# A matmul with layer normalisation: the fifth row tile's first quarter taken early, one quarter turned by VectorE, loads by quadrant

## The chip, the cores and the metric

The kernel runs on one core of a Trainium2 chip. The metric is the device time of one execution in microseconds, as the median of several runs. Five engines work side by side, each through its own queue of instructions: TensorE (PE) multiplies, VectorE (DVE) and ScalarE (ACT) work element by element, GpSimd (POOL) and SyncE (SP) issue most of the DMAs. Engines wait for one another by semaphores.

## The reference

With a and b of 2048 x 2048 in fp32:

```python
x = np.matmul(a, b)
mean = np.mean(x, axis=-1, keepdims=True)
var = np.var(x, axis=-1, keepdims=True)
normalized = (x - mean) / np.sqrt(var + eps)
return (gamma * normalized + beta).astype(np.float32)
```

Mean and variance of a row need the row's 2048 products complete, and the products need all of b.

## The kernel before

**Tiles.** Rows of a are cut into 16 row tiles of 128, numbered from 0, so tile 4 is the fifth. The columns of b are cut into 4 blocks of 512, and k into 16 k tiles of 128. A row tile has four *quarters* of k, of four k tiles each; (i, c) is quarter c of row tile i, and (i, q) is, for products, column block q of row tile i. One matmul (`mm`, L140) takes one k tile of one row tile as stationary operand, 128 x 128, and 512 columns of b, in fp16, and adds into one of the 8 PSUM banks. Row tiles 0 to 14 take 64 matmuls each, 960 in all; the last one has spans of its own (`products_last`).

**Ways to turn a.** The stationary operand needs k on the partitions. Row tiles 0 to 3 come as sixteen *pieces* (tile, quarter) of 128 x 512; each is cast to fp16 (`cast_first`), transposed by TensorE in four 128 x 128 steps into a PSUM bank (`turn_first`) and copied to `at` by VectorE (`keep_first`). Row tiles from 4 on are loaded so that each group of 32 partitions holds another 32-column part (`load_tile`: eight DMAs of 64 KB a half tile), cast by ScalarE (`cast_tile`), and turned in 32 x 32 blocks by VectorE (`transpose_part`, one quarter per instruction).

**Stages.** b arrives during the first 60 us, in left halves and right halves of each k tile (`load_b`), and is cast half by VectorE and half by ScalarE (`cast_left`, `cast_right`). Four row tiles work together meanwhile:

- the first K1 = 4 k tiles of the left two column blocks, then of the right two; the partial sums are put by in SBUF (`put_by`, ScalarE for even blocks, VectorE for odd ones);
- the other 12 k tiles of the left blocks, then of the right ones, each sum added to the part put by (`add_up`, VectorE), with its statistics (`stats`, VectorE) after it;
- then the loop over row tiles 4 to 14, 64 matmuls each, which also turns tile i + 2, normalises tile i - 1, and takes a half of one of the first four tiles (`normalise`: `centre` and `scale` on VectorE);
- the last row tile, with a shorter tail.

**Order.** The order of the work is written out by hand: the Python code is run once, and what it emits for an engine is that engine's queue, in that order. So a line that stands later in the code stands later in its engine's queue. The SP queue issues the loads of b and of row tiles 0 to 5, gamma, beta and the outputs; the POOL queue issues those of row tiles 6 to 15. A load also waits for a free buffer: `firstp` has 4 for a, `bigp` has 8 for b and the outputs.

**What the change touches.** The list of pieces (L89); the loads (L314 to L341); the end of the right first stage, where pieces 6 and 7 are turned (L409 to L426); the left second stage (L429 to L455), which turns pieces 8 to 15; the right second stage (L458 to L485), where tile 4's quarters are turned by VectorE among the additions and tile 5's after the statistics; and the loop (L487 to L508).

Of the kernel before, what the change touches and what calls it, by code (L numbers as in the profile page):

```python
# [9 lines left out]
FP32 = mybir.dt.float32  # L10
FP16 = mybir.dt.float16
# [4 lines left out]
def kernel(  # L16
# [16 lines left out]


    nc = tc.nc
    P = 128
# [15 lines left out]
    atp = ctx.enter_context(tc.tile_pool(name="atp", bufs=6))  # L52
    xpool = ctx.enter_context(tc.tile_pool(name="xpool", bufs=16))
    upool = ctx.enter_context(tc.tile_pool(name="upool", bufs=2))
# [33 lines left out]

    pieces = [(g, c) for c in range(4) for g in range(G)]  # L89

# [23 lines left out]

    def load_tile(i, h, queue):
        f = firstp.tile([P, 2, 4, P], FP32, tag="first", name=f"p{i}_{h}")
        for c in (0, 1):
            for q in range(4):
                queue.dma_start(  # L119
                    f[ds(32 * q, 32), c], a_pieces[q, 2 * h + c][:, ds(4 * i, 4)])  # L120
        tile_in[i, h] = f

    def cast_tile(i, h):
        a16 = a16p.tile([P, 2, 4, P], FP16, tag="a16", name=f"a{i}_{h}")
        nc.scalar.copy(a16, tile_in.pop((i, h)))  # L125
        tile_in[i, h] = a16

# [3 lines left out]
    def transpose_part(i, c):  # L131
        nc.vector.transpose(  # L132
            at[i][:, ds(4 * c, 4), :].rearrange("p t (j r) -> p j t r", r=32),
            tile_in[i, c // 2][:, c % 2].rearrange("p j (k t) -> p j t k", t=4),
        )
# [162 lines left out]
    with tc.manual_schedule(engines=order):  # L298
# [21 lines left out]
        for t in range(K1):  # L320
            load_b(t, 1)
            if t:
                load_first(K1 + t - 1)
        load_first(2 * K1 - 1)
        for t in range(K1, n_kt):
            load_b(t, 0)
            if K1 + t < n_kt:
                load_first(K1 + t)
        for t in range(K1, n_kt - 2):
            load_b(t, 1)  # L330
        load_tile(4, 0, nc.sync)
        for t in range(n_kt - 2, n_kt):
            load_b(t, 1)
        load_tile(4, 1, nc.sync)
        for h in (0, 1):
            load_tile(5, h, nc.sync)
        nc.sync.dma_start(gamma_b, gamma.unsqueeze(0).to_broadcast([P, N]))
        nc.sync.dma_start(beta_b, beta.unsqueeze(0).to_broadcast([P, N]))
        for i in range(6, n_mt):
            for h in (0, 1):  # L340
                load_tile(i, h, nc.gpsimd)  # L341

# [65 lines left out]
        bank(*late)  # L408
        cast_first(2 * K1 - 1)  # L409
        waits = list(range(K1))  # L410
        for j, (g, q) in enumerate(early):
            mm(g, q, K1 - 1, 0, K1)
            put_by(g, q)
            if j in (4, 6):
                n = K1 + j // 2
                turn_first(n)
                keep_first(n)
            if j in (1, 3, 5):
                mm(*late, waits.pop(0), 0, K1)
            if j == 2:  # L420
                cast_left(K1)
            if j == 5:
                cast_first(2 * K1)
        for t in waits:
            mm(*late, t, 0, K1)
        put_by(*late)  # L426


# [3 lines left out]
        for t in range(K1, n_kt - 3):  # L432
            n = K1 + t
            if t > K1:
                keep_first(n - 1)
            if K1 < t and n < n_kt:
                cast_first(n)
            cast_left(t + 1)
            for g, q in early[:5]:
                mm(g, q, t, K1)  # L440
            if n < n_kt:
                turn_first(n)
            for g, q in early[5:]:
                mm(g, q, t, K1)
        bank(*late)
        for t in range(n_kt - 2, n_kt):
            cast_left(t)
        for t in range(K1, n_kt - 3):
            mm(*late, t, K1)
        for j, (g, q) in enumerate(left):  # L450
# [7 lines left out]
        for g, q in right:  # L458
            bank(g, q)
        new_at(4)  # L460
        for t in range(K1 + 3, n_kt):
            if t == n_kt - 2:
                cast_tile(4, 0)
                transpose_part(4, 0)
                transpose_part(4, 1)
            cast_right(t)
            if t - K1 - 3 < len(left):
                stats(*left[t - K1 - 3])
        for t in range(K1, n_kt - 2):
            for g, q in right:  # L470
                mm(g, q, t, K1)
        cast_tile(4, 1)
        for j, (g, q) in enumerate(right):
            for t in (n_kt - 2, n_kt - 1):
                mm(g, q, t, K1)
            add_up(g, q)
            if j in (1, 3):
                transpose_part(4, 2 + j // 2)
        for g, q in right:
            stats(g, q)  # L480
        new_at(5)
        for c in range(4):
            if c % 2 == 0:
                cast_tile(5, c // 2)
            transpose_part(5, c)  # L485

        for i in range(G, last):  # L487
# [8 lines left out]
            for q in range(n_nb):  # L496
                bank(i, q)
                for t in range(n_kt):
                    mm(i, q, t)
                stats(i, q)  # L500
                if i + 2 < n_mt:
                    if q % 2 == 0:
                        cast_tile(i + 2, q // 2)
                    transpose_part(i + 2, q)
# [44 lines left out]
```

## Time and profile before

| | |
|---|---|
| median of 7 runs | 244.82 us (244.55 to 245.58) |
| the profiled execution's own time | 244.48 us |
| its span, first to last instruction | 242.7 us |
| TensorE busy | 232.6 us (96%) |
| VectorE busy | 197.5 us (81%) |
| ScalarE busy | 94.1 us (39%) |
| matmuls on row tiles 0 to 14 | 960 |
| transposes on TensorE (128 x 128) | 64 |
| turnings on VectorE, 0.689 us each | 48 |
| read from HBM, written | 35.65 MB, 16.78 MB |

Matmuls overlap in the pipeline, so a row's mean duration of one (379 ns) is longer than the time from one start to the next. A timeline line gives start and duration in microseconds, engine, line of the kernel, operation, output and input tile with shapes, how many instructions were merged, and in brackets the idle time before it with what ended it. Windows give, for each stretch, its length, busy time and number of instructions of TensorE, its weight loads, VectorE, ScalarE and GpSimd, then TensorE's granted clock as a share of the full one, the busy share of the DMA engines and GB/s.

### The profile page before, as it was taken

The page shows a single profiled execution, that of the slowest core. Times are in us where ns is not written, and L with a number is a line of the kernel's source. Part 1 is how long each engine was busy: PE and PEld are TensorE (multiplying, and loading weights), DVE is VectorE, ACT ScalarE, POOL GpSimd, SP SyncE. Part 2 cuts the span into 40 slices and gives each one's busy share as a digit, 9 for nine tenths or more (in the row PEclk, how much of TensorE's full clock was granted, in tenths as well). Part 3 has the DMA queues.
Part 4 walks back from the last instruction along what each step waited for, and adds up shares of the span by engine and source line. Part 5 has one row for each costly group of instructions (what it writes and reads, how often), then busy time and mean ns, then how long its engine had stood idle before and what let it go on. Part 6 is the DMA issues. An engine that isn't in the chain of part 4 may idle for free.

```text
span 242.7 us, 3388 instructions
## 1 busy us (share of the span) xinstructions
PE 232.6 (96%) x1137; PEld 108.5 (45%) x1137; DVE 197.5 (81%) x371; ACT 94.1 (39%) x167; POOL 89.2 (37%) x168
## 2 busy tenths in 40 slices
PE   8999999999999999999999999999999999999960
PEld 2445554444444444444444444444444444446440
DVE  1467865883599999998999899998999895966962
ACT  3474434443325130461909255370917391020020
POOL 0000000000776497798976707693670000000011
PEclk9999999999999999999999999999999999999996
DMA  6999999995989558586866726472584222030405
GB/s 177 402 404 402 399 402 409 406 328 170 258 218 314 161 171 274 188 281 131 259 205 230 224 97 242 166 276 86 209 214 185 90 86 89 35 138 0 176 0 173
DMA packets 22129, 52.66 MB, mean 217 GB/s; under 512 B 4448, under 2 KB 9056, under 8 KB 21856
## 3 DMA queue, kind: packets, MB, share of 16 engines
q1 hardware_dynamic: 16704, 41.74, 47.0%
q0 software_dynamic: 5120, 10.50, 16.9%
q8 instruction: 9, 0.15, 0.3%
q10 hardware_dynamic: 288, 0.21, 0.3%
q14 instruction: 8, 0.07, 0.1%
HBM read 35.65 MB, written 16.78 MB: 216 GB/s over the span
## 4 chain that ended last, share of the span: by engine, by line
PE 94%; DVE 3%; issue 0%; DVEq 0%
PE ps L141 84%; PE ps_last L230 6%; PE w_ps L306 3%; PE t_ps L109 2%; DVE x L154 1%; DVE c L287 1%; DVE at L113 0%; DVEq L544 0%; DVE b L86 0%; DVE ps_last L259 0%; DVE h L103 0%; DVE mv_last L272 0%; DVE bnst_last L249 0%; DVE warm L299 0%; DVE rs L173 0%
## 5 line engine op out<-in xcount | busy, mean ns | idle before, releaser
L141 PE MATMUL ps<-b,at 128*128 128x512 f16 x960 | 210.6, 379 | 0.5 <-DVE at L113 0.3
L141 PEld LDWEIGHTS <-at 128*128 128x128 f16 x960 | 93.0, 98 | 111.7 <-DVE at L113 1.7
L119 POOL DMA_DIRECT2D p<-in_a_dram x160 | 87.0, 551 | 93.2 <-DMA w<-in_b_dram 59.0
L183 DVE SCALAR_TENSOR_TENSOR c<-u,rs,beta_b 128x512 f32<-128x512 f32 x60 | 42.2, 745 | 0.0
L149 DVE BATCH_NORM_STATS2 bnst<-ps 128x6 f32<-128x512 f32 x44 | 29.8, 679 | 10.9 <-PE ps L141 10.8
L132 DVE STREAM_TRANSPOSE at<-a 128x512 f16<-128x512 f16 x48 | 32.8, 689 | 2.8 <-ACT a L125 2.8
L167 ACT ACTIVATE sq<-mv,eps_t 128x1 f32<-128x1 f32 x15 | 4.4, 295 | 76.4 <-DVE mv L165 76.4
L215 ACT ACTIVATE junk<-b 128x1024 f16<-128x1024 f16 x32 | 33.7, 1055 | 0.5
L177 DVE SCALAR_TENSOR_TENSOR u<-ps,mv,gamma_b 128x512 f32<-128x512 f32 x44 | 31.6, 743 | 0.4
L125 ACT CAST a<-p 128x1024 f16<-128x1024 f32 x24 | 24.8, 1039 | 12.3 <-DMA p<-in_a_dram 12.0
L269 POOL TENSOR_TENSOR u_last_n<-u_last_n,gamma_b 128x128 f32<-128x128 f32 x1 | 0.5, 454 | 53.4 <-ACT u_last_n L268 53.4
L82 ACT CAST b<-w 128x512 f16<-128x512 f32 x16 | 9.9, 620 | 15.5 <-DMA w<-in_b_dram 15.5
L87 ACT CAST b<-w 128x512 f16<-128x512 f32 x16 | 9.9, 621 | 11.9 <-DMA w<-in_b_dram 11.9
L230 PE MATMUL ps_last<-b,at 128*128 128x512 f16 (+4 forms) x96 | 14.1, 308 | 0.0
L160 DVE TENSOR_TENSOR x<-ps,x 128x512 f32<-128x512 f32 x16 | 10.1, 677 | 3.5 <-PE ps L141 3.5
L81 DVE CAST b<-w 128x512 f16<-128x512 f32 x16 | 6.8, 423 | 6.8 <-DMA w<-in_b_dram 6.6
L113 DVE COPY at<-t_ps 128x512 f16<-128x512 f16 x16 | 6.8, 423 | 6.7 <-PE t_ps L109 6.6
L177 DVE SCALAR_TENSOR_TENSOR u<-x,mv,gamma_b 128x512 f32<-128x512 f32 x16 | 11.4, 735 | 0.1
L230 PEld LDWEIGHTS <-at 128*128 128x128 f16 x96 | 8.8, 98 | 5.4
L149 DVE BATCH_NORM_STATS2 bnst<-x 128x6 f32<-128x512 f32 x16 | 10.3, 683 | 0.0
L86 DVE CAST b<-w 128x512 f16<-128x512 f32 x16 | 6.7, 416 | 2.8 <-DMA w<-in_b_dram 2.6
L306 PE MATMUL w_ps<-warm 128*128 128x512 f16 x17 | 6.7, 560 | 1.2 <-DVE warm L299 1.2
(40 smaller groups left out, 60.7 us busy)
## 6 DMA issues: line engine op xcount, KB each, us to landing
w<-in_b_dram SPq DMA_DIRECT2D x32, 512.0 KB, 8.6
out_dram<-c SPq DMA_DIRECT2D x30, 512.0 KB, 3.0
p<-in_a_dram POOLq DMA_DIRECT2D x160, 64.0 KB, 3.7
f<-in_a_dram SPq DMA_DIRECT2D x16, 256.0 KB, 7.8
p<-in_a_dram SPq DMA_DIRECT2D x32, 64.0 KB, 4.1
gamma_b<-in_gamma_dram SPq DMA_DIRECT2D x1, 1024.0 KB, 7.9
beta_b<-in_beta_dram SPq DMA_DIRECT2D x1, 1024.0 KB, 11.9
out_dram<-c SPq DMA_DIRECT2D x2, 256.0 KB, 2.5
```

Source lines behind the costliest of these rows:

```text
L82: nc.scalar.copy(b16[:, kt, NB:NH], w[:, NB:NH])
L119: queue.dma_start(f[ds(32 * q, 32), c], a_pieces[q, 2 * h + c][:, ds(4 * i, 4)])
L125: nc.scalar.copy(a16, tile_in.pop((i, h)))
L132: nc.vector.transpose(at[i][:, ds(4 * c, 4), :].rearrange("p t (j r) -> p j t r", r=32), tile_in[i, c // 2][:, c % 2].rearrange("p j (k t) ...
L141: nc.tensor.matmul(x_of[i, q], at[i][:, kt, :], b16[:, kt, ds(q * NB, NB)], start=(kt == lo), stop=(kt == hi - 1),)
L149: nc.vector.bn_stats(bnst[i][:, q, :], x_of[i, q])
L160: nc.vector.tensor_tensor(x, x_of[i, q], x, AluOp.add)
L177: nc.vector.scalar_tensor_tensor(u, x_of[i, q], mv_of[i][:, 0:1], gamma_b[:, ds(q * NB, NB)], AluOp.subtract, AluOp.mult,)
L183: nc.vector.scalar_tensor_tensor(c[:, ds(q % 2 * NB, NB)], u, rs_of[i], beta_b[:, ds(q * NB, NB)], AluOp.mult, AluOp.add,)
L215: nc.scalar.activation(junk, b16[:, kt, ds(h * NH, NH)], ActFn.Copy, accum_out=b_sum[:, h, kt:kt + 1])
L230: nc.tensor.matmul(x[:, 0:w], at[last][:, t, :], b16[:, t, ds(lo, w)], start=(t == 0), stop=(t == n_kt - 1))
L306: nc.tensor.matmul(w_ps, warm[:, 0:P], warm, start=True, stop=True)
```

## The change

Four things at once:

- Quarter 0 of row tile 4 is loaded, cast and turned early, and its 16 matmuls run right after the first stage of the right blocks; its four partial sums are put by. In the loop, tile 4 then takes k tiles 4 to 15 and adds the parts.
- Quarter 3 of row tiles 0 to 3 is no longer among the pieces (12 in place of 16). It is loaded by `load_pair`, cast by ScalarE and turned by VectorE in the left second stage.
- `load_pair` brings one quarter of two neighbouring row tiles with four DMAs of 128 KB. It is used for quarter 3 of tiles 0 to 3 and quarters 1 to 3 of tiles 4 and 5. b's last two right halves come ahead of tile 4's pairs on the SP queue.
- Casts and turnings go by quarter (`cast_part`). In the right second stage, quarters 1 and 2 of tile 4 are turned among the additions, quarter 3 after the statistics, followed by tile 5's four.

The eighth bank of the left second stage, (3, 1), is also begun at k tile 8 in place of the end. The diff, with a line of "..." where unchanged or renamed lines are left out:

```diff
-    xpool = ctx.enter_context(tc.tile_pool(name="xpool", bufs=16))
+    xpool = ctx.enter_context(tc.tile_pool(name="xpool", bufs=20))
...
-    pieces = [(g, c) for c in range(4) for g in range(G)]
+    pieces = [(g, c) for c in range(3) for g in range(G)]
...
-    def load_tile(i, h, queue):
-        f = firstp.tile([P, 2, 4, P], FP32, tag="first", name=f"p{i}_{h}")
-        for c in (0, 1):
-            for q in range(4):
-                queue.dma_start(
-                    f[ds(32 * q, 32), c], a_pieces[q, 2 * h + c][:, ds(4 * i, 4)])
-        tile_in[i, h] = f
-
-    def cast_tile(i, h):
-        a16 = a16p.tile([P, 2, 4, P], FP16, tag="a16", name=f"a{i}_{h}")
-        nc.scalar.copy(a16, tile_in.pop((i, h)))
-        tile_in[i, h] = a16
+    def new_parts(parts):
+        f = firstp.tile([P, 2, 4, P], FP32, tag="first", name="p%d_%d" % parts[0])
+        for j, x in enumerate(parts):
+            tile_in[x] = f[:, j]
+
+    def load_part(i, c, queue=None):
+        for q in range(4):
+            (queue or nc.sync).dma_start(
+                tile_in[i, c][ds(32 * q, 32)], a_pieces[q, c][:, ds(4 * i, 4)])
+
+    def load_pair(i, c):
+        f = firstp.tile([P, 8, P], FP32, tag="first", name=f"d{i}_{c}")
+        tile_in[i, c], tile_in[i + 1, c] = f[:, 0:4], f[:, 4:8]
+        for q in range(4):
+            nc.sync.dma_start(f[ds(32 * q, 32)], a_pieces[q, c][:, ds(4 * i, 8)])
+
+    def load_half(i, h, queue=None):
+        new_parts([(i, 2 * h), (i, 2 * h + 1)])
+        load_part(i, 2 * h, queue)
+        load_part(i, 2 * h + 1, queue)
+
+    def cast_part(i, c):
+        a16 = a16p.tile([P, 4, P], FP16, tag="a16", name=f"a{i}_{c}")
+        nc.scalar.copy(a16, tile_in[i, c])
+        tile_in[i, c] = a16
...
+        new_parts([(4, 0)])
+        load_part(4, 0)
         load_first(2 * K1 - 1)
         for t in range(K1, n_kt):
             load_b(t, 0)
-            if K1 + t < n_kt:
+            if K1 + t < len(pieces):
                 load_first(K1 + t)
-        for t in range(K1, n_kt - 2):
+            elif t in (9, 11):
+                load_pair(t - 9, 3)
+        for t in range(K1, n_kt):
             load_b(t, 1)
-        load_tile(4, 0, nc.sync)
-        for t in range(n_kt - 2, n_kt):
-            load_b(t, 1)
-        load_tile(4, 1, nc.sync)
-        for h in (0, 1):
-            load_tile(5, h, nc.sync)
+        for c in range(1, 4):
+            load_pair(4, c)
+        new_parts([(5, 0)])
+        load_part(5, 0)
...
         bank(*late)
-        cast_first(2 * K1 - 1)
         waits = list(range(K1))
         for j, (g, q) in enumerate(early):
             mm(g, q, K1 - 1, 0, K1)
             put_by(g, q)
-            if j in (4, 6):
-                n = K1 + j // 2
-                turn_first(n)
-                keep_first(n)
+            if j == 4:
+                turn_first(2 * K1 - 2)
+                keep_first(2 * K1 - 2)
             if j in (1, 3, 5):
                 mm(*late, waits.pop(0), 0, K1)
-            if j == 2:
-                cast_left(K1)
             if j == 5:
-                cast_first(2 * K1)
+                cast_part(4, 0)
+                new_at(4)
+                transpose_part(4, 0)
         for t in waits:
             mm(*late, t, 0, K1)
         put_by(*late)
+
+        for q in range(n_nb):
+            bank(4, q)
+        cast_first(2 * K1 - 1)
+        cast_left(K1)
+        cast_first(2 * K1)
+        for q in range(n_nb):
+            for t in range(K1):
+                mm(4, q, t, 0, K1)
+            if q == 1:
+                turn_first(2 * K1 - 1)
+                keep_first(2 * K1 - 1)
+            put_by(4, q)
...
         for t in range(K1, n_kt - 3):
             n = K1 + t
-            if t > K1:
+            if K1 < t <= 2 * K1:
                 keep_first(n - 1)
-            if K1 < t and n < n_kt:
+            if K1 < t < 2 * K1:
                 cast_first(n)
             cast_left(t + 1)
+            if t in (9, 11):
+                for g in (t - 9, t - 8):
+                    cast_part(g, 3)
+                    transpose_part(g, 3)
+            if t == 2 * K1:
+                bank(*late)
+                for u in range(K1, t):
+                    mm(*late, u, K1)
             for g, q in early[:5]:
                 mm(g, q, t, K1)
-            if n < n_kt:
+            if t < 2 * K1:
                 turn_first(n)
             for g, q in early[5:]:
                 mm(g, q, t, K1)
-        bank(*late)
+            if t >= 2 * K1:
+                mm(*late, t, K1)
         for t in range(n_kt - 2, n_kt):
             cast_left(t)
-        for t in range(K1, n_kt - 3):
-            mm(*late, t, K1)
...
-        new_at(4)
         for t in range(K1 + 3, n_kt):
-            if t == n_kt - 2:
-                cast_tile(4, 0)
-                transpose_part(4, 0)
-                transpose_part(4, 1)
             cast_right(t)
...
-        cast_tile(4, 1)
         for j, (g, q) in enumerate(right):
             for t in (n_kt - 2, n_kt - 1):
                 mm(g, q, t, K1)
             add_up(g, q)
             if j in (1, 3):
-                transpose_part(4, 2 + j // 2)
+                cast_part(4, 1 + j // 2)
+                transpose_part(4, 1 + j // 2)
         for g, q in right:
             stats(g, q)
+        cast_part(4, 3)
+        transpose_part(4, 3)
         new_at(5)
-        for c in range(4):
-            if c % 2 == 0:
-                cast_tile(5, c // 2)
+        for c in (1, 2, 3, 0):
+            cast_part(5, c)
             transpose_part(5, c)
...
             for q in range(n_nb):
                 bank(i, q)
-                for t in range(n_kt):
-                    mm(i, q, t)
+                lo = K1 if i == G else 0
+                for t in range(lo, n_kt):
+                    mm(i, q, t, lo)
+                if i == G:
+                    add_up(i, q)
                 stats(i, q)
                 if i + 2 < n_mt:
-                    if q % 2 == 0:
-                        cast_tile(i + 2, q // 2)
+                    cast_part(i + 2, q)
                     transpose_part(i + 2, q)
```

More of the change, by code (lines that the diff above doesn't have):

```diff
@@ L132, in transpose_part @@
         nc.vector.transpose(
-            at[i][:, ds(4 * c, 4), :].rearrange("p t (j r) -> p j t r", r=32),
-            tile_in[i, c // 2][:, c % 2].rearrange("p j (k t) -> p j t k", t=4),
+            at[i][:, ds(4 * c, 4), :].rearrange("p t (s r) -> p s t r", r=32),
+            tile_in[i, c].rearrange("p s (k t) -> p s t k", t=4),
         )
@@ L340 @@
             for h in (0, 1):
-                load_tile(i, h, nc.gpsimd)
+                load_half(i, h, nc.gpsimd)
         left = [(g, q) for g in range(G) for q in (0, 1)]
```

## The prediction

> **What bounds the kernel now.** I read the page's totals and chain first, then the timelines of TensorE and VectorE around the edited places, then the windows for the clock.
>
> ```profile
> span 242.7 us, 3388 instructions
> ...
> PE 94%; DVE 3%; issue 0%; DVEq 0%
> PE ps L141 84%; PE ps_last L230 6%; PE w_ps L306 3%; PE t_ps L109 2%; DVE x L154 1%; DVE c L287 1%; DVE at L113 0%; DVEq L544 0%; DVE b L86 0%; DVE ps_last L259 0%; DVE h L103 0%; DVE mv_last L272 0%; DVE bnst_last L249 0%; DVE warm L299 0%; DVE rs L173 0%
> ```
>
> TensorE carries 94% of the chain. Its timeline has no break after the opening:
>
> ```profile
> 24.30 0.39 PE L109 MATMUL t_ps<-ident,h 128*128 128x128 f16 x4
> 24.52 1.46 PE L141 MATMUL ps<-b,at 128*128 128x512 f16 x6
> ...
> 38.46 71.76 PE L141 MATMUL ps<-b,at 128*128 128x512 f16 x331
> ```
>
> 331 matmuls in 71.76 us are 0.216 us each, back to back; four transposes through PSUM take 0.22 us (24.30 to 24.52). So whatever delays TensorE after 18.5 us comes out at the end one for one, and TensorE gains only by what leaves its queue.
>
> VectorE's timeline where the four-row-tile stage hands over to the loop over single tiles, in start, duration and group:
>
> ```profile
> 65.58 1.29 DVE L160 TENSOR_TENSOR x<-ps,x 128x512 f32<-128x512 f32 x2 [2.70 <-PE ps L141]
> 67.20 0.71 DVE L132 STREAM_TRANSPOSE at<-a 128x512 f16<-128x512 f16 x1 [0.33 <-ACT a L125]
> 67.83 1.25 DVE L160 TENSOR_TENSOR x<-ps,x 128x512 f32<-128x512 f32 x2
> 69.01 0.69 DVE L132 STREAM_TRANSPOSE at<-a 128x512 f16<-128x512 f16 x1
> 69.62 2.45 DVE L160 TENSOR_TENSOR x<-ps,x 128x512 f32<-128x512 f32 x4
> 71.99 4.83 DVE L149 BATCH_NORM_STATS2 bnst<-x 128x6 f32<-128x512 f32 x8
> 76.73 2.48 DVE L132 STREAM_TRANSPOSE at<-a 128x512 f16<-128x512 f16 x4
> ```
>
> VectorE is full here and runs behind TensorE. Row tile 4 is not hurt, since all its turned quarters are done by 69.70 us, while its first matmul starts at 68.40 (instruction records) and its thirteenth, the first to read quarter 3, at 70.99. The eight statistics (71.99 to 76.73, 0.593 us each) and tile 5's four turnings come after.
>
> [...] the VectorE rows above stand in the order of the code, even where one idles (2.70 us). [...] the warm-up matmuls start 427 ns apart until 6.28 us and 216 ns apart after, and the clock falls within some 4 us of the last matmul:
>
> ```profile
> 234.40:238.40 4.00, 0.02 (x1) 0.00 (x0) 3.43 (x8) 1.47 (x4) 1.67 (x3) 1.00 0.28 98
> 238.50:242.60 4.10, 0.00 (x0) 0.00 (x0) 0.00 (x0) 0.00 (x0) 0.00 (x0) 0.50 0.45 150
> ```
>
> The clock column reads 1.00, then 0.50. Its records put the rise at 6.36 us and the fall at 238.46 us[...].
>
> **The change part by part.** The base is the profiled execution, 244.48 us (span 242.70 and 1.78 around it), 0.34 below the median of 244.82; differences are added to the median.
>
> 1. *Sixteen transposes fewer on TensorE* (pieces 12 to 15, four each): 4 x 0.222 = 0.89 us gained. Their VectorE work (four casts at 0.42, four copies at 0.42: 3.4 us) gives way to four turnings at 0.69 (2.8 us) and four ScalarE casts; both engines wait for DMA at 36 to 43 us in the trace, which hides them.
>
> 2. *Sixteen matmuls of tile 4 run early.* The matmuls stay 960, so TensorE's sum is unchanged. The gain could only be filled waits, and of those between 18.5 and 68.4 us I find 0.28 us (two gaps at 26.4 and 26.8 us, for banks); I take these as gone. VectorE gets two more copies (0.69) early and four more additions (0.68, 2.7 us) in tile 4's loop. That loop's VectorE work starts after its share of item 3's wait and lies beside matmuls: three instructions of 0.6 us a group against 12 x 0.216 = 2.6 us.
>
>    New wait: the first early matmul needs quarter 0 turned. On ScalarE its cast stands behind put_by(2, 2), on VectorE the turning behind put_by(2, 3). Before, put_by(2, 3) ran here:
>
> ```profile
> 24.42 0.68 DVE L154 COPY x<-ps 128x512 f32<-128x512 f32 x1
> ```
>
> Without the cast_left that stood ahead it starts about 24.2 and the next instruction about 24.8. The cast ends about then too (matmuls of (2, 2) end at 23.59, then 0.59 copy and 0.62 cast). Turning 0.69: done 25.5. TensorE, without the transposes of piece 7, is there at 24.51. Wait 1.0 us; bounds 0 (overlap) and 1.4 (a DMA-late part). Bank (3, 1) at t = 8 waits for the copy of piece 11: 0.07 us.
>
> 3. *Quarter 3 of tile 4 is turned after the eight statistics.* In the built order, VectorE has 8 additions and 2 turnings, 8 statistics, then quarter 3. Counted from the first addition, which TensorE releases as before (65.58): 8 x 0.593 + 2 x 0.61 + 8 x 0.593 + 0.69 = 11.4 us, so 76.99, and 0.04 for the signal: 77.03. TensorE starts tile 4 at 68.40, has eight matmuls that need quarters 1 and 2, and meets quarter 3 at 68.40 + 8 x 0.216 = 70.13. It waits **6.9 us**. A common shift of both moves nothing. Queued behind are tile 4's other 40 matmuls, tile 5 and all the rest. Bounds 6.3 to 7.3.
>
> 4. *The clock.* [...] 1.7 to 3.3, middle 2.4 us. [...]
>
> 5. *Loads.* The fifth tile's part and the pairs come in 512-byte packets (27 ns in the records, 84 ns for 2048 bytes: 0.86 us for 256 KB instead of 0.67; 1 MB of pairs 3.5 instead of 2.7). [...] With 256 KB more ahead of b, the last left half lands at about 42.1 + 0.86 + 0.8 = 43.7 us; TensorE, 3.4 us later, needs it at 46. Hidden; without that cover, up to 1.6 us. SP's queue has b's last two right halves ahead of tile 4's pairs now; the pairs land by about 64 us, used from 69. POOL's queue, which waits for a buffer that a cast of tile 5 empties, starts tile 6 at about 62 instead of 60.6 us: hidden. gamma and beta follow on SP's queue, behind fewer and larger DMAs than now (beta is issued at 72.08 us and lands some 12 us later, about when the first centring runs at 84.15): earlier if anything.
>
> 6. *Smaller casts.* ScalarE casts quarters (0.62 us for 512 columns) instead of halves (1.04): 4 x 0.62 - 2 x 1.04 = 0.4 us more a row tile on an engine that is 39% busy: hidden; without cover 0.4 us. The four further buffers for partial sums cost space alone.
>
> Sum: -0.89 + 1.0 - 0.28 + 0.07 + 6.9 + 2.4 = +9.2. 244.82 + 9.2 = **254.0 us**.
>
> **The rivals.** *No clock loss* (the gap is shorter, or the fall comes late): 244.82 + 6.8 = 251.6. For it: the fall at the end took 4.05 us from the last matmul[...].
>
> *A second wait*: tile 4's extra additions push VectorE, 96 of 100 us busy from 100 to 200, past TensorE, which then waits for PSUM banks; or b comes late after all. 2.7 us more work at most, or 1.6 us: 255.6 to 257. Against: item 3's idle time lets VectorE catch up by 6.9 us first, and the bank that tile 6 takes is freed by tile 4's addition, earlier than by its centring.
>
> *VectorE meets TensorE's ninth matmul in time*: the other side. Place: quarter 3 ahead of the ninth matmul. If its turning ran where its input is there (about 64 us, ahead of the additions), nothing would be waited for and only the 0.89 and 0.28 would show, with or without the 1.0: 243.7 to 244.8. It decides at 6.9 us: so much would have to leave VectorE between 65.6 and 77. The durations are measured and the queue doesn't reorder, so little speaks for it. That the early matmuls fill TensorE's waits can't do this either: there are only 0.28 us of them.
>
> **How the numbers follow.** The likeliest case 0.80 (252.5 to 255.5), no clock loss 0.10, a second wait 0.06, the other side 0.04. 254.0 is the first case's. The range of 250.8 to 256.0 takes in the second and half of the third and leaves out under 1 in 10 by cases, a little more for sizes that I have wrong. Faster, same, slower by 0.2% (0.5 us, about what this kernel's runs can tell): 0.03, 0.02, 0.95.
>
> **What would show it.** The chain or TensorE's timeline breaks eight matmuls into the second part of tile 4, for 6 to 7 us, ended by VectorE's transposition; the clock column shows 0.50 for some 3 to 7 us over that place; a wait of about 1 us before the first early matmul; 48 transposes through PSUM; no wait for b. Times would scatter more than the 1.0 us of before[...]. I am wrong if quarter 3 is turned before the statistics, or if TensorE shows no break there.

## The result, and the profile after

The changed kernel took **258.11 us** (median of 12 runs, 254.24 to 261.68) against 244.77 us for the kernel before (31 runs, 243.81 to 245.58): ratio **1.050**, 95% interval 1.047 to 1.052. The median takes all twelve runs, the ratio only the six within 1.5% of the fastest (254.24 to 257.93). The prediction was 254.0, with a range of 250.8 to 256.0: right in direction, 4 us short. The profiled execution took 257.93 us, 13.45 more than the one before. Its page, the lines that answer to those shown of before:

```profile
span 256.1 us, 3363 instructions
...
PE 76%; DMA 13%; DVE 7%; SPq 1%; ACT 0%; issue 0%; DVEq 0%; ACTq 0%
PE ps L155 70%; DMA w<-in_b_dram 7%; DMA f<-in_a_dram 6%; PE ps_last L244 5%; DVE x L174 2%; DVE bnst L163 2%; DVE x L168 1%; DVE at L146 1%; DVE c L301 1%; PE t_ps L110 0%; SPq L77 0%; DVE at L114 0%; SPq L99 0%; DVEq L577 0%; ACT h L104 0%
```

Before, no DMA stood on the chain. Now the arrivals of b (w) and of a's pieces (f) hold 13% of it. That is the surprise; it comes ahead of the wait that was predicted. TensorE's timeline, start and duration, with the idle time before in brackets:

```profile
24.15 1.03 PE L155 MATMUL ps<-b,at 128*128 128x512 f16 x4
26.05 1.90 PE L155 MATMUL ps<-b,at 128*128 128x512 f16 x8 [0.87 <-DVE at L146]
...
36.24 5.16 PE L155 MATMUL ps<-b,at 128*128 128x512 f16 x22
41.57 1.89 PE L155 MATMUL ps<-b,at 128*128 128x512 f16 x8 [0.18 <-DVE b L82]
43.92 1.89 PE L155 MATMUL ps<-b,at 128*128 128x512 f16 x8 [0.47 <-DVE b L82]
47.44 1.02 PE L155 MATMUL ps<-b,at 128*128 128x512 f16 x4 [1.63 <-DVE b L82]
48.90 1.63 PE L155 MATMUL ps<-b,at 128*128 128x512 f16 x6 [0.44 <-DVE at L146]
51.28 27.59 PE L155 MATMUL ps<-b,at 128*128 128x512 f16 x126 [0.75 <-DVE b L82]
85.55 24.72 PE L155 MATMUL ps<-b,at 128*128 128x512 f16 x107 [6.69 <-DVE at L146]
```

Three things stand here: the wait for quarter 0 of tile 4 (ended 26.05), five breaks from 41 to 51 us for b and for quarter 3 of the first tiles, and 6.69 us ahead of tile 4's ninth matmul (85.55). The brackets count from the modelled end of a matmul. To make a ledger I use the instruction records instead: the time from one matmul's start to the next, less the 0.216 us of back-to-back matmuls.

| us of TensorE's time, after minus before | predicted | measured |
|---|---|---|
| sixteen transposes fewer | -0.89 | -0.89 (48 transposes) |
| wait for quarter 0 of tile 4 | +1.0 | +1.04 (matmuls start 24.80, then 26.05) |
| gaps for banks at 26 us gone | -0.28 | -0.28 |
| bank (3, 1) begun at k tile 8 | +0.07 | +0.25 |
| waits in the left second stage | 0 | **+4.43** (0.34, 0.63, 1.79, 0.60, 0.15, 0.92) |
| wait for quarter 3 of tile 4 | +6.9 | +6.85 (78.49, then 85.55) |
| half clock | +2.4 | +1.44 (7 starts 0.21 late) |
| opening, the start and small gaps | 0 | +0.60 |
| sum | +9.2 | +13.4 |

The last matmul starts 13.44 us later than before (247.64 for 234.20), so the ledger holds all of it. The largest miss is one row.

VectorE around the second break:

```profile
74.06 1.29 DVE L174 TENSOR_TENSOR x<-ps,x 128x512 f32<-128x512 f32 x2 [5.23 <-PE ps L155]
75.27 0.71 DVE L146 STREAM_TRANSPOSE at<-a 128x512 f16<-128x512 f16 x1
75.90 1.26 DVE L174 TENSOR_TENSOR x<-ps,x 128x512 f32<-128x512 f32 x2
77.07 0.70 DVE L146 STREAM_TRANSPOSE at<-a 128x512 f16<-128x512 f16 x1
77.68 2.46 DVE L174 TENSOR_TENSOR x<-ps,x 128x512 f32<-128x512 f32 x4
80.05 4.84 DVE L163 BATCH_NORM_STATS2 bnst<-x 128x6 f32<-128x512 f32 x8
84.79 3.08 DVE L146 STREAM_TRANSPOSE at<-a 128x512 f16<-128x512 f16 x5
```

Eight additions, two turnings, eight statistics, then quarter 3 at 84.79, the first of five turnings: the order and the 11.4 us that the prediction counted, begun 8.5 us later than before (74.06 for 65.58), since TensorE is 5 us late and has tile 4's sixteen early matmuls, 3.5 us, behind it. The clock stood at 0.50 for 6.83 us, from 81.71 to 88.54. Three windows of half that length, of which the last two are this stretch (length, busy time of TensorE, its weight loads, VectorE, ScalarE, GpSimd, granted clock, DMA share, GB/s):

```profile
78.30:81.71 3.41, 0.57 (x3) 0.07 (x1) 3.41 (x7) 0.00 (x0) 2.56 (x5) 1.00 0.98 300
81.72:85.12 3.40, 0.00 (x0) 0.00 (x0) 3.40 (x7) 0.62 (x1) 2.41 (x5) 0.50 0.22 64
85.13:88.53 3.40, 2.98 (x8) 1.05 (x9) 3.37 (x7) 1.24 (x2) 3.40 (x7) 0.50 0.47 124
```

It fell after the first, in which TensorE had still worked 0.57 us, and rose after the third, of which TensorE had worked 2.98 us. So matmuls ran at half clock for 2.99 us, from 85.55 to 88.54.

Where b went late, the same windows of the changed kernel:

```profile
35.00:40.00 5.00, 4.92 (x27) 2.29 (x26) 1.56 (x5) 0.75 (x2) 0.00 (x0) 1.00 1.12 272
40.00:45.00 5.00, 4.36 (x20) 1.78 (x19) 2.04 (x4) 2.28 (x4) 0.00 (x0) 1.00 1.11 241
```

and of the kernel before:

```profile
35.00:40.00 5.00, 5.00 (x33) 2.56 (x31) 3.22 (x8) 1.73 (x3) 0.00 (x0) 1.00 1.03 407
40.00:45.00 5.00, 5.00 (x25) 2.29 (x24) 2.60 (x6) 1.99 (x4) 0.00 (x0) 1.00 1.02 405
```

The DMA engines are as busy in both (last column but one), but move 241 to 272 GB/s instead of 405 to 407. From 15 to 35 us it is 295 to 348 against 400 to 404. So b's last left half is cast at 50.80 us in place of 42.08; the prediction had 43.7 for its landing. Packets of b (4096 bytes) took 194 ns on average from 14 to 46 us, against 165 before, and those of the new loads (512 bytes) 47 ns, where the prediction put 27. The medians are 165 and 164: some of b's packets became much slower, not all of them a little.

### The profile page after: what moved, and what is told of

Read it like the earlier page. It is cut to its first block, busy times and chain, and to the rows that moved or that the text cites. A ratio compares the mean times of both kernels' runs of the same rounds, so it can differ in the third digit from the quotient of the medians.

```text
span 256.1 us, 3363 instructions
## 1 busy us (share of the span) xinstructions
PE 234.6 (92%) x1121; PEld 107.4 (42%) x1121; DVE 201.4 (79%) x373; ACT 97.1 (38%) x197; POOL 88.9 (35%) x168
## 4 chain that ended last, share of the span: by engine, by line
PE 76%; DMA 13%; DVE 7%; SPq 1%; ACT 0%; issue 0%; DVEq 0%; ACTq 0%
PE ps L155 70%; DMA w<-in_b_dram 7%; DMA f<-in_a_dram 6%; PE ps_last L244 5%; DVE x L174 2%; DVE bnst L163 2%; DVE x L168 1%; DVE at L146 1%; DVE c L301 1%; PE t_ps L110 0%; SPq L77 0%; DVE at L114 0%; SPq L99 0%; DVEq L577 0%; ACT h L104 0%
## 5 line engine op out<-in xcount | busy, mean ns | idle before, releaser
L146 DVE STREAM_TRANSPOSE at<-a 128x512 f16<-128x512 f16 x52 | 35.4, 691 | 1.5 <-ACT a L139 1.5
L163 DVE BATCH_NORM_STATS2 bnst<-ps 128x6 f32<-128x512 f32 x40 | 27.1, 680 | 10.5 <-PE ps L155 10.5
L191 DVE SCALAR_TENSOR_TENSOR u<-ps,mv,gamma_b 128x512 f32<-128x512 f32 x40 | 28.7, 743 | 0.4
L139 ACT CAST a<-p 128x512 f16<-128x512 f32 x42 | 25.2, 606 | 9.5 <-DMA p<-in_a_dram 7.4
L174 DVE TENSOR_TENSOR x<-ps,x 128x512 f32<-128x512 f32 x20 | 12.9, 684 | 7.7 <-PE ps L155 7.7
L191 DVE SCALAR_TENSOR_TENSOR u<-x,mv,gamma_b 128x512 f32<-128x512 f32 x20 | 14.3, 736 | 0.2
L163 DVE BATCH_NORM_STATS2 bnst<-x 128x6 f32<-128x512 f32 x20 | 13.1, 691 | 0.1
L114 DVE COPY at<-t_ps 128x512 f16<-128x512 f16 x12 | 5.1, 425 | 6.9 <-PE t_ps L110 6.8
L168 DVE COPY x<-ps 128x512 f32<-128x512 f32 x10 | 6.7, 684 | 1.9 <-PE ps L155 1.9
## 6 DMA issues: line engine op xcount, KB each, us to landing
f<-in_a_dram SPq DMA_DIRECT2D x12, 256.0 KB, 6.9
```

Source lines behind the costliest of these rows:

```text
L139: nc.scalar.copy(a16, tile_in[i, c])
L146: nc.vector.transpose(at[i][:, ds(4 * c, 4), :].rearrange("p t (s r) -> p s t r", r=32), tile_in[i, c].rearrange("p s (k t) -> p s t k", t=4),
L163: nc.vector.bn_stats(bnst[i][:, q, :], x_of[i, q])
L174: nc.vector.tensor_tensor(x, x_of[i, q], x, AluOp.add)
L191: nc.vector.scalar_tensor_tensor(u, x_of[i, q], mv_of[i][:, 0:1], gamma_b[:, ds(q * NB, NB)], AluOp.subtract, AluOp.mult,)
```

## The experiments

The theories of the 6.9 us and of the clock come from the prediction; the loads needed new ones. Each load of `load_pair` and `load_part` writes 32 neighbouring partitions in pieces of 512 bytes (128 columns of a: each group of 32 partitions holds another 128-column part of the quarter, not a 32-column one as "Ways to turn a" says). So it may be the *size* of the pieces, the *number* of loads in the queue (in the traces of both kernels at most 8 of SP's are between issue and landing at once), or the *place* they are written to. All diffs are against the changed kernel unless another is named.

**The order: quarter 3 ahead of the statistics.**

```diff
-            if j in (1, 3):
-                cast_part(4, 1 + j // 2)
-                transpose_part(4, 1 + j // 2)
+            if j in (1, 2, 4):
+                c = {1: 1, 2: 2, 4: 3}[j]
+                cast_part(4, c)
+                transpose_part(4, c)
...
-        cast_part(4, 3)
-        transpose_part(4, 3)
         new_at(5)
```

> The changed kernel with one move: tile 4's quarters are cast and turned after additions 1, 2 and 4 (quarter 3 after addition 4), none after the eight statistics. Order theory (the wait of 6.85 us at tile 4's ninth matmul, and the half clock behind it, come from quarter 3 standing behind the statistics): both go, 258.1 - 6.85 - 1.4 = 249.9, up to 1 us more if the turning is still a little late; no break over 1.5 us at the ninth matmul and no half clock there. Rival (VectorE is behind TensorE there anyway, and a wait of the same size shows at the next bank or at tile 5's quarters): 256 to 258. The waits for b ahead of it stay (4.4 us in the profile of the changed kernel).

Measured: 251.18 us (248.88 to 252.24), ratio 1.024 (1.018 to 1.030). The second break is all but gone:

```profile
80.31 19.88 PE L155 MATMUL ps<-b,at 128*128 128x512 f16 x90 [0.23 <-DVE at L146]
```

By starts it is 0.39 us instead of 6.85, and the clock stays at 1.00 through it. What remains over the kernel before is waits of 5.9 us in the left second stage of this profile (4.43 in the changed kernel's); that difference is about the 1.3 us by which the time exceeds the forecast. By the trace the order costs what was said, and the loads, or what hangs on them, cost some 6 us more.

**The loads: width, then size.** First to all 128 partitions, in the same pieces of 512 bytes:

```diff
+    a_rows = a.rearrange("(i p) k -> p i k", p=P)
...
-            nc.sync.dma_start(f[ds(32 * q, 32)], a_pieces[q, c][:, ds(4 * i, 8)])
+            nc.sync.dma_start(
+                f[:, ds(2 * q, 2)], a_rows[:, ds(i, 2), ds(512 * c + P * q, P)])
```

(and `load_part` likewise)

> The changed kernel with SP's loads of tile 4's quarter 0 and of the pairs written to all 128 partitions by each DMA, in the same 512-byte pieces of the same rows, the same number of DMAs and bytes, in the same places of the queue. It turns other data, so quarter 3 of tiles 0 to 3 and quarters of tiles 4 and 5 are not those of the reference; the amount of work is the same. Narrow theory (a DMA that writes only 32 partitions slows itself and the loads of b beside it): rate from 35 to 45 us back from 241 to 272 GB/s to 350 or more, the waits for b shrink from 4.4 to under 1.5 us, time about 254. Small theory (512-byte packets are slow in themselves) and in-flight theory (eight DMAs are under way at most, and eight small ones hold too few bytes): unchanged, 257 to 259.

Measured: 253.52 us, ratio 1.035 (1.033 to 1.038). TensorE runs from 36.06 to the second break without a stop:

```profile
36.06 38.18 PE L162 MATMUL ps<-b,at 128*128 128x512 f16 x174
80.93 19.41 PE L162 MATMUL ps<-b,at 128*128 128x512 f16 x81 [6.69 <-DVE at L153]
```

and the windows over the same stretch show the rate back (371 GB/s at 30 to 35 us):

```profile
35.00:40.00 5.00, 4.92 (x27) 2.29 (x26) 3.41 (x8) 2.18 (x4) 0.00 (x0) 1.00 1.08 367
40.00:45.00 5.00, 5.00 (x25) 2.29 (x24) 2.38 (x5) 2.80 (x5) 0.00 (x0) 1.00 1.03 410
```

512 bytes take 31 ns here, b's packets 165 ns: as many loads and pieces of the same size, from the same rows and columns of a, and no wait for b. Neither the size nor the number of loads is it. The counter-test keeps 32 partitions and makes the pieces four times as large:

```diff
+            nc.sync.dma_start(
+                f[ds(32 * q, 32)].rearrange("p (x s) k -> p x (s k)", x=2),
+                a[ds(P * i + 64 * q, 64), ts(c, 512)].rearrange("(p x) k -> p x k", x=2))
```

(and `load_part` likewise, here and in the next two)

> The changed kernel with the same SP loads still written to 32 partitions per DMA, but in 2048-byte pieces; same number of DMAs and bytes, same places in the queue. Other rows go to other partitions, so those quarters are not the reference's; the amount of work is the same. Small theory: packets cost as the 2048-byte ones of the pieces (84 ns), the waits for b go, about 254. Narrow theory: still slow, rate from 35 to 45 us under 300 GB/s, 257 to 259 or more. In-flight theory: unchanged, 257 to 259.

Measured: 258.27 us, ratio 1.055 (1.052 to 1.057), as slow as the changed kernel, with 3.3 us of waits in the left second stage, 2.8 us of half clock (1.4 in the changed kernel's profile) and the low rate, which here ends earlier:

```profile
35.00:40.00 5.00, 4.92 (x27) 2.29 (x25) 1.04 (x3) 0.62 (x1) 0.00 (x0) 1.00 0.95 250
40.00:45.00 5.00, 4.51 (x21) 1.84 (x19) 2.07 (x4) 2.18 (x4) 0.00 (x0) 1.00 1.01 356
```

So it is in the main where the pieces go; whether larger pieces give a little relief (328 GB/s from 15 to 45 us, against 299) this run can't tell. Next, half the partitions a load instead of a quarter:

```diff
+    a_rows = a.rearrange("(i p) k -> p i k", p=64)
...
+            nc.sync.dma_start(
+                f[ds(64 * (q % 2), 64), ds(4 * (q // 2), 4)],
+                a_rows[:, ds(2 * i, 4), ds(512 * c + P * q, P)])
```

> As the run with all 128 partitions, but each of SP's loads of tile 4's quarter 0 and of the pairs writes 64 partitions, in 512-byte pieces; same DMAs, bytes and rows, other data in quarters as there. Narrow theory with a contended share of the write side: between the two, rate from 35 to 45 us about 300 to 350 GB/s, time 254 to 256. If only fewer than 64 partitions hurt: 253.5. If anything short of all 128 hurts alike: 258.

Measured: 257.81 us (256.10 to 259.98), ratio 1.050 (1.045 to 1.055): 64 neighbouring partitions are no better than 32.

```profile
35.00:40.00 5.00, 4.92 (x27) 2.29 (x25) 1.52 (x5) 0.62 (x1) 0.00 (x0) 1.00 1.09 238
40.00:45.00 5.00, 4.32 (x21) 1.75 (x19) 2.06 (x4) 2.27 (x4) 0.00 (x0) 1.00 1.11 248
```

**Width or place.** That 64 equals 32 leaves two readings: only a load to all 128 partitions spares its neighbours (the width), or it matters which partitions a load writes (the place). Loads to 32 partitions again, but every fourth one, tell them apart. If the place counts, the first forecast holds, if the width, the second:

```diff
-            nc.sync.dma_start(f[ds(32 * q, 32)], a_pieces[q, c][:, ds(4 * i, 8)])
+            nc.sync.dma_start(f[q:P:4], a_pieces[q, c][:, ds(4 * i, 8)])
```

> The changed kernel with the four loads of each part and pair on SP's queue going to every fourth partition (q, q+4, ... q+124) instead of 32 neighbouring ones. Rows read, pieces of 512 bytes, bytes, number of loads, 32 partitions a load and order are those of the changed kernel; the data arrive on other partitions than the turning expects, so the output is not the reference's. [...] b is in time as with the loads to all 128 partitions, no wait for b in the left half's second stage, over 365 GB/s at 35 to 45 us; 253.5 us as there. Theory of the width (any load to fewer than all 128 partitions slows its neighbours): waits of 3 to 6 us for b and 240 to 275 GB/s, 257 to 259 us.

Measured: **253.59 us** (252.97 to 254.71), ratio 1.037 (1.034 to 1.040), the time of the loads to 128 partitions. No wait in the left second stage, and the rate is there:

```profile
35.36 38.18 PE L159 MATMUL ps<-b,at 128*128 128x512 f16 x174
```

```profile
35.00:40.00 5.00, 4.92 (x27) 2.29 (x26) 2.80 (x6) 2.18 (x4) 0.00 (x0) 1.00 1.08 366
40.00:45.00 5.00, 5.00 (x25) 2.28 (x24) 2.38 (x5) 2.79 (x5) 0.00 (x0) 1.00 1.03 410
```

512 bytes took 30 ns, b's packets 165, and the loads of the pairs landed 5.6 us after their issue (median), where those of the changed kernel took 8.4. Source, sizes, numbers and partitions per load are those of the changed kernel; only which partitions differs. The width falls, the place stands. What it is in the place that counts is not shown: other sets of 32 partitions were not run.

**Fewer of these loads.** Sixteen pieces again, no pairs of quarter 3 of the first tiles, the eighth bank back at its old place; all else as changed:

```diff
-    pieces = [(g, c) for c in range(3) for g in range(G)]
+    pieces = [(g, c) for c in range(4) for g in range(G)]
...
-            elif t in (9, 11):
-                load_pair(t - 9, 3)
```

> The changed kernel with one part undone: quarter 3 of tiles 0 to 3 are pieces again (loads of 256 KB, 64 transposes on TensorE), tile 4's early quarter and the rest stay. All three load theories: the pairs are gone from among b's left halves, so the waits for b in the left second stage fall from 4.4 us to under 1 us, for 0.89 us more of transposes: 258.1 - 3.5 to 4.4 + 0.9 = 254.6 to 255.5. Rival (b is late because of tile 4's part at 13 to 18 us and of the slot releases that wait for TensorE, not of the pairs): waits for b stay over 2 us, 257 to 259. The wait at tile 4's ninth matmul stays near 6.9 us.

Measured: 254.90 us, ratio 1.041 (1.038 to 1.043). No waits for b and 404 to 410 GB/s from 30 to 50 us, so of the early loads it is the pairs, 1 MB of them, that delay b; the part of tile 4 (0.26 MB, at about 15 us) is absorbed. The break ahead of tile 4's ninth matmul is unchanged at 6.85 us, but the half clock lasted 10.2 us here (6.83 in the changed kernel) and cost 2.9 us, so the time is above the 253.5 us of the loads to 128 and to every fourth partition.

**The clock.** 28 matmuls of zeros into a spare bank, between tile 4's eighth and ninth:

```diff
                 for t in range(lo, n_kt):
+                    if i == G and q == 0 and t == 12:
+                        f_ps = psum.tile([P, NB], FP32, tag="c_ps", bufs=8, name="f_ps")
+                        for _ in range(28):
+                            nc.tensor.matmul(f_ps, warm[:, 0:P], warm, start=True, stop=True)
                     mm(i, q, t, lo)
```

> The changed kernel with 28 matmuls of a zero tile, 28 x 0.216 = 6.05 us, put into TensorE's queue ahead of tile 4's ninth matmul, that is into its wait of 6.85 us. Clock theory (the idle wait lets the clock fall to half, and 1.4 us are lost behind it): the wait shrinks to about 0.8 us, the clock column stays at 1.00 there, and TensorE is 1.4 us or more shorter from the ninth matmul on: 258.1 - 1.4 = 256.7. Rival (the clock falls for another reason, or costs nothing): 258.1, or more if the matmuls add to the wait.

Measured: 256.77 us (254.65 to 258.32), ratio 1.048 (1.043 to 1.053). The times don't tell it from the changed kernel, whose runs spread over 7 us. The trace does: the clock stays at 1.00,

```profile
77.00:86.00 9.00, 8.35 (x40) 3.46 (x38) 9.00 (x16) 2.42 (x5) 7.16 (x14) 1.00 0.67 231
```

and from the ninth matmul's start to the last it is 160.62 us instead of 162.09, 1.47 less: the 1.44 of the ledger.

**Can the loads be mended?** First, in the kernel with the earlier turnings, the order of the four loads in `load_part` and `load_pair`:

```diff
-        for q in range(4):
+        for q in (0, 2, 1, 3):
```

> The kernel with the turnings before the statistics (251.2 us, waits for b 5.9 us in its profile) with the four loads of each part and pair issued in the order of quadrants 0, 2, 1, 3[...]. Same data, same result. If several loads of the queue are in flight together[...]: waits for b under 3 us, 246 to 249 us. If the loads go through one after the other, or the engines stay in step, nothing changes: 250 to 252 us, waits for b of 4 to 6 us.

Measured: 251.18 us (248.35 to 252.45), ratio 1.028 (1.025 to 1.031). The median is that of the kernel it edits and the intervals overlap. Its profile, of its fastest run, has 3.3 us of waits where the other's has 5.9, and 264 GB/s at 35 to 40 us, so the loads are still slow; whether the order gives a small relief is not settled.

The next three carry the mended order of the turnings: tile 4's quarters 1 to 3 ahead of the right second stage, quarter 0 cast after the first `put_by` and turned after the second instead of both after the sixth. They differ in the loads. The first two also take bank (3, 1) after the matmuls of all seven other groups at k tile 8; they write all partitions at once, 64 KB a load, from a source of three dimensions (quadrant, row, column), shared between SP and GpSimd or all on SP:

```diff
+    def wide(f, i, c, s):
+        (nc.gpsimd if s % 2 else nc.sync).dma_start(f, a_pieces[:, c, :, 4 * i + s])
...
-        for q in range(4):
-            nc.sync.dma_start(f[ds(32 * q, 32)], a_pieces[q, c][:, ds(4 * i, 8)])
+        for s in range(8):
+            wide(f[:, s], i, c, s)
```

> The changed kernel mended where its losses were: SP's loads of turned quarters take one 128-partition DMA of 64 KB per group of 32 rows (four quadrants at once, same data as the change), every second one issued by GpSimd; tile 4's quarters 1 to 3 are turned ahead of the additions, and its quarter 0 is cast and turned two and four groups earlier in the right first stage. It computes the reference. Theory (order, clock, narrow loads and the early wait are all of the loss): 0.89 us of transposes are gained and little else is lost: 243.6 to 244.6, at or just under the kernel before. Rival (b is late even so, since the 512-byte pieces take 0.8 us more for each MB and the early matmuls cannot cover it, or the many small DMAs hold b up): 245.5 to 249, with waits for b between 40 and 52 us.

Measured: 260.75 us, ratio 1.066 (1.063 to 1.069), far above the forecast and its rival. b is later than in the changed kernel (one wait of 6.9 us), at 145 to 246 GB/s from 30 to 45 us. With all on SP (`nc.sync` throughout):

> As the mended kernel, but all of these 64 KB loads are issued by SP. In-flight theory (small DMAs in SP's queue, eight under way at a time, starve the engines even when they are wide): a pair takes 8 issues of about 0.36 us = 2.9 us for 512 KB where 1.3 us would do, so b comes some 3 to 4 us later than in the mended kernel, about what the early matmuls cover: 244 to 247, slower than the mended one by 0.5 us or more. If only narrow writes matter: the same as the mended kernel within 0.3 us.

Measured: 265.39 us, ratio 1.083 (1.081 to 1.084), again far above the forecast. The queue's own timeline:

```profile
27.32 8.54 SPq L122 DMA_DIRECT2D d<-in_a_dram  x8
35.90 1.21 SPq L77 DMA_DIRECT2D w<-in_b_dram  x2
37.21 9.14 SPq L122 DMA_DIRECT2D d<-in_a_dram  x8
```

Eight issues took SP 8.5 and 9.1 us (0.53 to 2.67 us each in the whole run, against 0.33 for one of b's when nothing holds it), and b's loads stand behind them. The packets themselves are quick, 32 ns for 512 bytes, but the DMA engines lack work:

```profile
40.00:45.00 5.00, 2.23 (x8) 0.79 (x7) 1.62 (x3) 2.18 (x4) 0.00 (x0) 0.88 0.35 113
```

A share of 0.35 is between 5 and 6 of the 16 engines. By the packet records, at most 7 of these packets were under way at once, where the loads by row of the second experiment had up to 20 from 33 to 36 us. From 73 to 87 us SP issued them back to back, one every 0.80 us, and the packets kept pace, at 79 GB/s with no load of b beside them; TensorE stood still for 7.4 us, until 90.21, behind an addition whose place in VectorE's queue is after turnings that waited for them. Whether SP is slow to issue a load of this form, or waits because it runs on few engines, no run separates.

Then the pairs of quarter 3 as changed, by quadrants, but issued by GpSimd:

```diff
+            (nc.gpsimd if c == 3 and i < 4 else nc.sync).dma_start(
+                f[ds(32 * q, 32)], a_pieces[q, c][:, ds(4 * i, 8)])
```

> Computes the reference. The changed kernel with the same two mends of order, and its two pairs among b's left halves, still by quadrant, issued by GpSimd in place of SP, so that their packets mix with b's over a longer time and take no place among SP's eight. If mixing relieves the narrow writes: waits for b under 1.5 us, 243.8 to 245.5. If narrow writes cost the same wherever they are issued: waits for b of 3 to 5 us stay, 248 to 251.

Measured: 252.11 us (251.34 to 254.17), ratio 1.032 (1.029 to 1.035), 1 us above the forecast for loads that cost the same wherever they are issued. Another queue brings the loads, and the delay, earlier:

```profile
38.21 2.29 PE L156 MATMUL ps<-b,at 128*128 128x512 f16 x5 [2.79 <-DVE b L82]
```

b's loads issued from 24 us on landed 13 to 16 us later, at 248 to 261 GB/s from 30 to 40 us.

**Does this close the account?** The mended order with loads to all 128 partitions by row (the data are those of the second experiment):

> The run with all 128 partitions per load (other data in the turned quarters, same work), and besides tile 4's quarters 1 to 3 turned ahead of the additions and its quarter 0 cast and turned two and four groups earlier. Theory (order, the clock behind it, narrow loads and the early wait are all of the loss, and the sixteen transposes fewer are a gain): 253.5 - 6.86 - 1.8 - 1.04 = 243.8, that is 0.4% under the kernel before. Rival (the sixteen transposes are paid back elsewhere, by VectorE's further work or by waits for banks): 244.8 or more.

Measured: 244.47 us (22 runs) against 244.60, ratio **0.9991** (0.9982 to 1.0000), 0.7 us above the forecast and 0.3 below the rival's. And the mended order with sixteen pieces, where tile 4's loads stay by quadrant:

> Computes the reference. The run with sixteen pieces (quarter 3 of tiles 0 to 3 again transposed by TensorE), with the same two mends of order. Theory: 254.9 - 6.85 - 2.9 - 1.03 = 244.1, and at most 0.3% from the kernel before, since no transpose is saved. Rival (the early quarter of tile 4 or the casts by quarter cost something of their own): 245.5 or more.

Measured: 245.12 us (22 runs), ratio **1.0020** (1.0009 to 1.0031), between the forecast and its rival as well. The two timelines run through both places, first by row, then with sixteen pieces:

```profile
35.31 75.01 PE L162 MATMUL ps<-b,at 128*128 128x512 f16 x345
```

```profile
42.42 67.81 PE L155 MATMUL ps<-b,at 128*128 128x512 f16 x312
```

With the order and the loads mended, the 13 us are gone. Of the 0.89 us of the sixteen transposes little is left in the first: its last matmul starts 0.33 us earlier than before (233.87 for 234.20), since its trace has a new wait of 0.43 us ahead of piece 7's transposes (26.18, then 26.82) and one of 0.25 for the bank. No version with all data in their place beat the kernel before. Not tried: a load that spreads the right data over all 128 partitions in one or two issues.

## Why the prediction was wrong, and where it was right

**Item 5, "Loads", failed.** "Hidden; without that cover, up to 1.6 us" became 4.43 us. The step priced the loads by packets of 512 bytes at 27 ns, the row of a stretch without b, and put 43.7 us for b's last left half; it was cast at 50.80. The runs show in its place that what counts is which partitions are written: beside b, the same packets take 47 ns into 32 neighbouring partitions and 30 ns into every fourth. And the loss is not theirs alone. From 15 to 45 us the six windows average 299 GB/s, against 403 before: 3.1 MB less, worth 7.7 us. As an estimate, the 2560 narrow packets at 47 ns held the 16 engines for 7.5 us, where their 1.31 MB at 403 GB/s would take 3.3: 4.2 us; b's 1561 packets at 194 ns for 165 add 2.9. An entry of the trace before had the clue: from 50 to 54 us, where quadrant loads mix with b, 512 bytes took 43 ns and 4096 bytes 181. The pairs of tile 4, put at 64 us, landed from 69 to 75, still ahead of their turnings.

Of the 4.43 us, 3.68 end with VectorE's cast of b; the 0.60 at 48.90 and the 0.15 at 49.49 end with turnings of quarter 3, whose casts stand behind b's late ones in ScalarE's queue. "VectorE meets TensorE's ninth matmul" didn't happen; "a second wait", given 0.06, did, by its clause that b comes late, at nearly three times its price.

**Item 4, the clock: right that it falls, size off.** 2.4 us became 1.44. The 2.4 and its range were the author's estimate of how long matmuls would run at half clock; no trace of before shows such a break. Here the fall came 3.2 us after the eighth matmul's start, and the rise 2.99 us after the ninth's. With the wait filled by matmuls, the clock stayed at 1.00 and 1.47 us came back, so the loss hangs on the wait. The smaller cost took 1 us off the sum, so the loads alone were missed by more than the total shows. In other runs of the same break the cost was 1.8 to 2.9 us, so the range of 1.7 to 3.3 was too high at its low end alone.

**Item 3, right**: 6.9 predicted, 6.85 measured in the changed kernel and 6.85 to 6.86 in five other runs of that order. A common shift moved nothing, as said: TensorE came 5 us late and the wait stayed.

**Items 1 and 2, right**: 0.89, and 1.04 for 1.0; the 0.28 was won, the bank cost 0.25 for 0.07. In the kernel with mended order and loads to 128 partitions the wait for quarter 0 is gone, and what stood behind it, piece 7's transposes, wait 0.43 us for VectorE's cast.

**Item 6**: ScalarE's smaller casts show in no wait of their own. The scatter was foretold (7 us, where the kernel before has 1.8), but the cost of the half clock, 1.4 to 2.9 us in the profiles of this break, gives only a part of it. The waits in the left second stage were 4.4, 5.15 and 5.9 us in three profiles (as changed, with the filling matmuls, with the earlier turnings) whose code is the same up to there; what sets their size from run to run is open.

## What to carry to other kernels

Before a load is called hidden, look at which partitions it writes: here packets into 32 neighbouring ones took 47 ns, where those into every fourth took 30, and those of the full-width loads beside them 194, where they took 165 before. The busy share in the DMA column (1.11 to 1.12, where 1.02 to 1.03 before) doesn't show it, the GB/s beside it do (241 to 272 for 405 to 407). Where a wait must be counted, count it as here, from the event that releases both sides, so that shifts cancel. And a load that is rewritten to write all partitions is only better if it still keeps the DMA engines supplied: the loads from a three-dimensional source wrote all 128, the DMA share fell to 0.35, and the kernel took 265.4 us with them where the narrow loads, with the same order of the turnings, took 252.1.

## What the runs showed of the hardware that was not expected

- **Which partitions a load writes.** Loads of 512-byte pieces to 32 or 64 neighbouring partitions beside b: 238 to 272 GB/s together at 35 to 45 us, and 250 at 35 to 40 us (356 at 40 to 45) with pieces of 2048 bytes. To 128 partitions, or to every fourth: 366 to 410. Where the kernel before has narrow loads with almost nothing of b beside them (56 to 58 us, 57 GB/s) they took 28 ns. That full-width packets in flight beside narrow ones grow from 165 to 194 ns is measured here; through what they are held back is not.
- **How long half clock lasts.** In the changed kernel the clock stood at 0.50 for 6.83 us, and TensorE worked 2.98 us of the 3.41 before it rose. With sixteen pieces it was still at 0.50 after a stretch of that length with 2.56 us of work:

```profile
80.87:84.27 3.40, 2.56 (x7) 0.91 (x8) 3.40 (x7) 1.34 (x3) 3.12 (x6) 0.50 0.27 94
84.29:87.68 3.39, 3.39 (x10) 1.18 (x9) 1.61 (x3) 1.99 (x3) 3.39 (x8) 0.50 0.39 122
```

  With loads to 64 partitions, the waits for b left TensorE 1.26 us of work in 3.41 us, and half clock followed:

```profile
45.62:49.03 3.41, 1.26 (x6) 0.35 (x5) 1.25 (x3) 2.00 (x4) 0.00 (x0) 1.00 1.03 412
49.04:52.44 3.40, 3.40 (x9) 1.15 (x10) 1.82 (x5) 1.70 (x4) 0.00 (x0) 0.50 1.03 410
```

  What sets the moments of the fall and the rise is not shown.

- **A wide load can be slow too.** A load of 64 KB as [128, 128] from a source of three dimensions held SP for 0.53 to 2.67 us, median 0.76, where b's 512 KB are issued in 0.33 when nothing holds them, and such loads alone moved 79 GB/s. What sets this is open.
